# Statistics of the last layer norm: four row tiles from VectorE to two accumulating ScalarE passes each

## The chip, the cores and the metric

The kernel runs on one core of one Trainium2 chip. Its time is the device time of one execution in microseconds (us), and the median of the runs is compared. The core has five engines with a queue of instructions each: TensorE (PE in the profile; PEld is its weight load), VectorE (DVE), ScalarE (ACT), GpSimd (POOL) and SyncE (SP), which here only issues DMA transfers. An engine works through its own queue in order and waits for the others by semaphores.

## What is computed

The kernel is one layer of a hybrid decoder trunk on a sequence of 1024 positions with 1024 channels, in float32. Two token mixers and an output projection come first; they are not touched. The change concerns the end:

```python
def layer_norm(x, g, b):
    mu = jnp.mean(x, axis=-1, keepdims=True)
    var = jnp.mean(jnp.square(x - mu), axis=-1, keepdims=True)
    return (x - mu) * lax.rsqrt(var + LN_EPS) * g + b

def conv_ffn(h, w_up, dw_w, dw_b, w_down):
    u = causal_dwconv(h @ w_up, dw_w, dw_b)
    gate, val = jnp.split(u, 2, axis=-1)
    return (jax.nn.silu(gate) * val) @ w_down      # inner width 2816

h = layer_norm(DN_ALPHA * h + mix, ln1_g, ln1_b)
ffn = conv_ffn(h, w_up, dw_w, dw_b, w_down)
h = layer_norm(DN_ALPHA * h + ffn, ln2_g, ln2_b)   # the last norm, the kernel's output
```

## The kernel before, in words

A matrix product in float32 precision is done as three products of rounded operands: high part by high part (line 190), high by low (191) and low by high (192). So each weight tile is first cast by ScalarE into its high part (L1251 in the last stage), and then VectorE subtracts the high part from the original for the low part (L1252). The matmuls of lines 191 and 192 wait for that subtraction.

The last stage is `down()`, the product with `w_down`. It is done by Strassen's scheme in its seven-product form: the table `products` lists seven block products p = 0 to 6, each over NK = 11 steps k. A product adds up in four of the eight PSUM banks, X (`acc` in the profile) or Y (`sm`), one bank for each of four row blocks t of 128 positions; a step is 4 x 3 = 12 matmuls of 128x512. The function `load(p, k)` brings the operands of a step: the activations from scratch by SyncE (L1212), the weight block by SyncE (L1215), and, where a product needs a sum of two blocks, a second operand by GpSimd's queue (L1219) and an addition on VectorE (L1184). Then come the cast and the subtraction. The raw tiles, called `dr_1`, `dr_2` and so on, rotate through five buffers; the split tiles, called `w_dn<p>_<k>`, through six.

When a product is complete, a function of the table adds its banks to the residual rows. The rows lie in eight tiles of 128x1024: tiles 0 to 3 in `rows03`, tiles 4 to 7 in `rows47`; E is their first half of 512 columns, L their second. After product 1, `two(t)` completes half E of tiles 0 to 3 (L1272). After product 5, `four(t)` completes half L of the same tiles and ends them: `ln_out`. After product 6, `three(t)` completes half E of tiles 4 to 7 (L1269) and ends these. So tiles 0 to 3 are finished beside the matmuls of product 6, and tiles 4 to 7 as their banks come out at the end. In product 6 the last eight steps are done bank by bank, so that the four banks are complete one after another; the last four of its weight tiles (`last`) are loaded long ahead.

The last norm of a tile goes like this. When a half of the row is complete, `ln_part` takes its statistics (BN_STATS, L231, 128x512). `ln_stats` joins the two halves' statistics into mean and variance (BN_AGGR, L250), ScalarE takes the root of the variance plus eps (L251), and VectorE its reciprocal (L254). `ln_apply` goes over each half twice: minus mean, times gain (L258); times reciprocal root, plus bias (L261). A half of the result then leaves by SyncE (L1335).

The order of each engine's queue is not that of the code. The instructions are recorded by a layer that sorts them by priorities (`high_priority` raises those of the weight loads by 4000 and those of tile 7's norm by 200) and by its own estimate of when operands are ready; it also sets the waits. So an instruction that is taken out can move others.

Of the kernel before, what the change touches and what calls it, by code (L numbers as in the profile page):

```python
# [8 lines left out]
F32 = mybir.dt.float32  # L9
F32R = mybir.dt.float32r  # L10
AF = mybir.ActivationFunctionType
ALU = mybir.AluOpType
# [4 lines left out]
P = 128  # L17
D = 1024
T = 1024
HALF = 512  # L20
# [41 lines left out]
def kernel(  # L62
# [17 lines left out]
    V, A, G, TE, SY = nc.vector, nc.scalar, nc.gpsimd, nc.tensor, nc.sync  # L80

    def pool(name, bufs=1, **kw):
        return tc.tile_pool(name=name, bufs=bufs, reuse_waits="tile", **kw)
# [11 lines left out]
    def bank(which):  # L95
# [16 lines left out]
    eps = const.tile([P, 1], F32, name="eps")  # L112
# [3 lines left out]
        out=quads, in_=ident.rearrange("p (j h) -> p h j", j=4), axis=AX.X, op=ALU.add  # L116
# [113 lines left out]
    def ln_part(pl, t, st, q):  # L230
        return V.bn_stats(out=st[:, q, :], in_=t[:, q * 512 : (q + 1) * 512])  # L231

    def ln_stats(pl, tiles, name, sts=None, keep=None):

        n = len(tiles)
        if keep is None:
            mv = pl.tile([P, n, 2], F32, tag="ln_mv", bufs=2, name=f"mv_{name}")
            rs = pl.tile([P, n], F32, tag="ln_rs", bufs=2, name=f"rs_{name}")
        else:
            mv, rs = keep  # L240
        for i, t in enumerate(tiles):
            if sts:
                st = sts[i]
            else:
                st = pl.tile([P, 2, 6], F32, tag="ln_st", bufs=2, name=f"st_{name}{i}")
                for q in range(2):
                    part = ln_part(pl, t, st, q)
                    if keep is not None:
                        parts_of.append(part)
            V.bn_aggr(out=mv[:, i, :], in_=st)  # L250
        root = A.activation(out=rs, in_=mv[:, :, 1], func=AF.Sqrt, bias=eps)  # L251
        if keep is not None:
            in_order.append(root)
        V.reciprocal(out=rs, in_=rs)  # L254
        return mv, rs

    def ln_apply(t, mv, rs, i, g, b):
        one = V.scalar_tensor_tensor(  # L258
            out=t, in0=t, scalar=mv[:, i, 0:1], in1=g, op0=ALU.subtract, op1=ALU.mult
        )  # L260
        two = V.scalar_tensor_tensor(  # L261
            out=t, in0=t, scalar=rs[:, i : i + 1], in1=b, op0=ALU.mult, op1=ALU.add
        )
        return one, two
# [875 lines left out]
    def down(upp, dp):  # L1140
# [20 lines left out]
        ]  # L1161
        c4.append(upp.tile([P, HALF], F32, tag="s3", name="c4_last"))
        rs = [r[:, t * D : (t + 1) * D] for r in (rows03, rows47) for t in range(4)]
        sts = [dp.tile([P, 2, 6], F32, name=f"st_f{t}") for t in range(8)]
        g, b = (dp.tile([P, D], F32, name=n) for n in ("ln2_g", "ln2_b"))
        first_own = dp.tile([P, 2, D], F32R, tag="w", bufs=3, name="w_dn_own")

# [103 lines left out]
        def more(ps, r, cs, op):  # L1271
            V.tensor_tensor(out=r[:, cs], in0=r[:, cs], in1=ps, op=op)  # L1272
# [3 lines left out]

        def two(t):
            more(Y[t], rs[t], E, ALU.add)
            ln_part(dp, rs[t], sts[t], 0)

        def six(t):
            own(X[t], rs[t], L, ALU.subtract)
# [7 lines left out]

        def four(t):
            more(Y[t], rs[t], L, ALU.add)
            ln_part(dp, rs[t], sts[t], 1)
            ln_out(upp, t, rs[t], g, b, sts[t])

        def three(t):
            own(X[t], rs[4 + t], E, ALU.add)
            ln_part(dp, rs[4 + t], sts[4 + t], 0)
            ln_out(upp, 4 + t, rs[4 + t], g, b, sts[4 + t])

        products = (
            (X, True, one),
            (Y, True, two),
            (X, False, six),
            (Y, True, seven),
            (X, False, five),
            (Y, False, four),
            (X, False, three),
        )
# [15 lines left out]
                    block(banks[t], ws[k], t, first, k)  # L1325
                then(t)

    def ln_out(dp, t, r, g, b, st):

        with tc.high_priority(offset=200 if t == 7 else 0):  # L1330
            mv, rstd = ln_stats(dp, [r], f"f{t}", [st])
            halves = [slice(q * HALF, (q + 1) * HALF) for q in range(2)]
            for cs in halves:
                ln_apply(r[:, cs], mv, rstd, 0, g[:, cs], b[:, cs])
                SY.dma_start(out[t * P : (t + 1) * P, cs], r[:, cs])  # L1335

    warm(46)
# [3 lines left out]
    with pool("rows0") as pl:  # L1341
        rs = [pl.tile([P, D], F32, name=f"r0_{t}") for t in range(4)]
# [20 lines left out]
    upp = ctx.enter_context(pool("up"))  # L1363
# [4 lines left out]
    ffn_stack.close()  # L1368
    dp = ctx.enter_context(pool("down", side="right"))
    down(upp, dp)  # L1370


# [98 lines left out]
```

## Time and profile before

| what | value |
|---|---|
| median of 3 runs | 1940.59 us (1940.09 to 1940.99) |
| profiled execution, its own time | 1940.01 us |
| span of the profile, first to last instruction | 1937.9 us |
| granted TensorE clock, mean | 0.999 |
| DVE busy, 1779 to 1790 us | 10.24 of 11.00 us |
| ACT busy, 1897 to 1938 us | 6.51 of 41.00 us |
| BN_STATS of the last norm (L231) | 16, 682 ns each |
| BN_AGGR of the last norm (L250) | 8, 202 ns each |

Rows of the timeline give start and duration in us, the engine, the line, the operation, the output and inputs by the program's names without numbers, and the count that is merged into the row; in brackets stands how long the engine sat idle before it and who ended that. Neighbours on an engine overlap a little, so the step from start to start is shorter than a duration. A row of the waits gives the total, the count and the longest in us. A row of a group gives busy us in total, mean ns of one, then idle time before them.

### The profile page before, as it was taken

To read this page: it belongs to the slowest core of one execution; us is meant where nothing else is said; L and a number is where in the kernel's file an instruction comes from. 1 tells how busy PE (TensorE), PEld (TensorE's weight loads), DVE (VectorE), ACT (ScalarE), POOL (GpSimd) and SP (SyncE) were. 2 spreads that over 40 slices of the span, in tenths; PEclk is the share of its full clock that TensorE was granted. 3 is DMA by queue.
4 is the path that set the end of the run, shared out by engine and by line. 5 is a ranking of instruction groups with operands and counts; after the bars stand their busy time and mean duration, and the time that the engine had idled before them with its cause. 6 is when DMAs were issued, how large, how long until landed. Compare 5 with 4: busy or idle time off the path is not lost.

```text
span 1937.9 us, 25802 instructions
## 1 busy us (share of the span) xinstructions
PE 1921.9 (99%) x9424; PEld 1570.3 (81%) x9424; DVE 1607.4 (83%) x2242; ACT 1084.2 (56%) x1626; POOL 217.1 (11%) x256
## 2 busy tenths in 40 slices
PE   9999999999999999999999999999999999999998
PEld 8888877788888788888888888888888888888886
DVE  7599999999887639899999546587788888889778
ACT  6676767763353366776765435365555555543542
POOL 1001010112300001111112040001000000122010
PEclk9999999999999999999999999999999999999999
DMA  6655555547356665656544644566455555479673
GB/s 218 219 172 201 173 205 177 166 166 270 130 182 222 211 207 183 202 180 212 176 168 163 213 151 131 181 243 228 163 168 185 179 182 186 157 281 360 198 245 112
DMA packets 127216, 376.27 MB, mean 194 GB/s; under 512 B 15184, under 2 KB 15728, under 8 KB 127088
## 3 DMA queue, kind: packets, MB, share of 16 engines
q1 hardware_dynamic: 107424, 318.48, 48.7%
q0 software_dynamic: 13184, 44.59, 6.6%
q10 hardware_dynamic: 6480, 11.55, 1.6%
q8 instruction: 74, 1.21, 0.3%
q14 instruction: 54, 0.44, 0.1%
HBM read 290.00 MB, written 84.56 MB: 193 GB/s over the span
## 4 chain that ended last, share of the span: by engine, by line
PE 79%; DVE 16%; ACT 2%; issue 2%; DMA 1%; POOL 0%; DVEq 0%; ACTq 0%; POOLq 0%
PE acc L192 18%; PE acc L191 18%; PE acc L190 18%; PE sm L190 7%; PE sm L191 7%; PE sm L192 7%; DVE c L558 6%; DVE x L511 2%; DVE w_c L161 2%; PE sm L647 1%; DMA st_wo<-wo 1%; PE sm L655 1%; PE sm L650 1%; DVE m L642 1%; DVE x L665 1%
## 5 line engine op out<-in xcount | busy, mean ns | idle before, releaser
L192 PE MATMUL acc<-hT_h,w_c 128*128 128x512 f32 x1000 | 391.4, 392 | 0.5 <-DVE w_c L161 0.5
L190 PE MATMUL acc<-hT_h,w_c 128*128 128x512 f32 x1000 | 391.1, 391 | 0.2 <-ACT zs L575 0.2
L191 PE MATMUL acc<-hT_l,w_c 128*128 128x512 f32 x1000 | 391.1, 391 | 0.0
L558 DVE SCALAR_TENSOR_TENSOR c<-v,pc,c 128x512 f32<-128x512 f32 x480 | 373.0, 803 | 7.0 <-ACT c L547 4.5
L190 PEld LDWEIGHTS acc<-hT_h,w_c 128*128 128x128 f32 x1000 | 187.8, 188 | 41.3 <-issue 1.9
L192 PEld LDWEIGHTS acc<-hT_h,w_c 128*128 128x128 f32 x1000 | 187.8, 188 | 40.9 <-issue 1.5
L191 PEld LDWEIGHTS acc<-hT_l,w_c 128*128 128x128 f32 x1000 | 187.8, 188 | 39.4 <-issue 1.1
L156 ACT CAST w_c<-st_c 128x1024 fp32r<-128x1024 f32 x128 | 133.8, 1046 | 111.2 <-PE acc L192 83.8
L626 POOL TENSOR_TENSOR ce<-ce,xbc 128x1024 f32<-128x1024 f32 x28 | 78.5, 2805 | 690.3 <-ACT ce L625 690.3
L1251 ACT CAST w_dn<-dr 128x1024 fp32r<-128x1024 f32 (+1 forms) x72 | 67.3, 942 | 73.4 <-DVE dr L1184 36.4
L190 PE MATMUL sm<-h1s,w_s 128*128 128x512 f32 x264 | 102.8, 389 | 0.5 <-ACT fuv L1094 0.5
L191 PE MATMUL sm<-h1s,w_s 128*128 128x512 f32 x264 | 102.7, 389 | 0.0
L192 PE MATMUL sm<-h1s,w_s 128*128 128x512 f32 x264 | 102.2, 389 | 0.0
L615 ACT ACTIVATE m<-ab,acs 128x128 f32<-128x128 f32 x256 | 78.3, 389 | 41.2 <-PE sm L647 39.1
L161 DVE TENSOR_TENSOR w_c<-st_c,w_c 128x1024 fp32r<-128x1024 f32 x62 | 78.9, 1273 | 17.6 <-ACT w_c L156 17.4
L511 DVE SCALAR_TENSOR_TENSOR x<-u,pc,x 128x512 f32<-128x512 f32 x96 | 78.6, 832 | 5.7 <-ACT x L509 5.6
L1252 DVE TENSOR_TENSOR w_dn<-dr,w_dn 128x1024 fp32r<-128x1024 f32 (+1 forms) x72 | 77.8, 1086 | 2.8 <-ACT w_dn L1251 2.6
L192 PE MATMUL acc<-h1b_h,w_ue 128*128 128x512 f32 x176 | 68.9, 395 | 0.3 <-DVE w_ue L161 0.3
L190 PE MATMUL acc<-h1b_h,w_ue 128*128 128x512 f32 x176 | 68.7, 390 | 0.0
L191 PE MATMUL acc<-h1b_l,w_ue 128*128 128x512 f32 x176 | 68.5, 389 | 0.0
L190 PE MATMUL sm<-h1b_h,w_s 128*128 128x512 f32 x176 | 68.5, 389 | 0.0
L191 PE MATMUL sm<-h1b_l,w_s 128*128 128x512 f32 x176 | 68.5, 389 | 0.0
(360 smaller groups left out, 4541.9 us busy)
## 6 DMA issues: line engine op xcount, KB each, us to landing
st_c<-wcol SPq DMA_DIRECT2D x128, 512.0 KB, 4.5
low_scr<-w_c SPq DMA_DIRECT2D x64, 512.0 KB, 2.9
w_c<-low_scr SPq DMA_DIRECT2D x64, 512.0 KB, 4.2
ab<-acs_scr SPq DMA_DIRECT2D x32, 512.0 KB, 4.2
dr<-wdown SPq DMA_DIRECT2D x55, 256.0 KB, 4.8
st_wo<-wo SPq DMA_DIRECT2D x24, 512.0 KB, 4.2
st_ue<-wup SPq DMA_DIRECT2D x22, 512.0 KB, 3.7
first_scr<-first ACTq DMA_DIRECT2D x44, 256.0 KB, 3.0
```

The lines of the kernel that those rows point to most:

```text
L156: casts.append(A.copy(w[:, 0, :], st))
L161: sub.tensor_tensor(out=w[:, 1, :], in0=st, in1=w[:, 0, :].bitcast(F32), op=ALU.subtract)
L190: TE.matmul(ps, wa(0), xa(0), start=start, stop=False, skip_group_check=more)
L191: TE.matmul(ps, wa(0), xa(1), start=False, stop=False, skip_group_check=more)
L192: TE.matmul(ps, wa(1), xa(0), start=False, stop=stop, skip_group_check=more)
L511: V.scalar_tensor_tensor(out=o, in0=u[:, k : k + HALF], scalar=pc[:, wc + k : wc + k + 1], in1=o, op0=ALU.mult, op1=ALU.add,)
L558: V.scalar_tensor_tensor(out=accs[i], in0=v[:, k : k + HALF], scalar=pc[:, wc + k : wc + k + 1], in1=accs[i], op0=ALU.mult, op1=ALU.add,)
L615: A.activation(out=m[:, h, :], in_=ab[:, h, :], func=AF.Relu, scale=-1.0, bias=acs[:, c, 8 * g + h : 8 * g + h + 1],)
L626: G.tensor_tensor(out=ce, in0=ce, in1=CT[:, cs].unsqueeze(1).to_broadcast([P, 8, P]), op=ALU.mult)
L642: V.tensor_tensor(out=m, in0=m, in1=cbm.unsqueeze(1).to_broadcast([P, 8, P]), op=ALU.mult)
L1251: A.copy(w[:, 0, cs], src)
L1252: V.tensor_tensor(out=w[:, 1, cs], in0=src, in1=w[:, 0, cs].bitcast(F32), op=ALU.subtract)
```

## The change

Tiles 0 to 3 no longer get BN_STATS and BN_AGGR on VectorE. Instead `ln_out` has ScalarE go over the finished row of 1024 twice. The first pass writes the row times −1/1024 to a scratch tile and adds it up in its accumulator, which gives minus the mean (L1337 of the changed kernel). The second pass squares the row plus that number and adds up the squares (L1340). The root is taken of the sum times 1/1024 plus eps (L1341); the reciprocal stays on VectorE (L1342). The two passes of `ln_apply` are now written in `ln_out` (L1344 and L1347), with "plus minus the mean" in place of "minus the mean". Tiles 4 to 7 keep their statistics as they were.

```diff
         def two(t):
             more(Y[t], rs[t], E, ALU.add)
-            ln_part(dp, rs[t], sts[t], 0)
...
         def four(t):
             more(Y[t], rs[t], L, ALU.add)
-            ln_part(dp, rs[t], sts[t], 1)
-            ln_out(upp, t, rs[t], g, b, sts[t])
+            ln_out(upp, t, rs[t], g, b)
...
-    def ln_out(dp, t, r, g, b, st):
+    def ln_out(dp, t, r, g, b, st=None):
...
+            if st is not None:
+                mv, rstd = ln_stats(dp, [r], f"f{t}", [st])
+                mean, op, rstd = mv[:, 0, 0:1], ALU.subtract, rstd[:, 0:1]
+            else:
+                sums = dp.tile([P, 3], F32, tag="ln_sums", bufs=2, name=f"sums_f{t}")
+                mean, op, square, rstd = sums[:, 0:1], ALU.add, sums[:, 1:2], sums[:, 2:3]
+                out_of = dp.tile([P, T + 32], F32, tag="u", bufs=3, name=f"sq_f{t}")
+                A.activation(
+                    out=out_of[:, :D], in_=r, func=AF.Identity, scale=-1.0 / D, accum_out=mean
+                )
+                A.activation(out=out_of[:, :D], in_=r, func=AF.Square, bias=mean, accum_out=square)
+                A.activation(out=rstd, in_=square, func=AF.Sqrt, bias=eps, scale=1.0 / D)
+                V.reciprocal(out=rstd, in_=rstd)
             for cs in halves:
-                ln_apply(r[:, cs], mv, rstd, 0, g[:, cs], b[:, cs])
+                V.scalar_tensor_tensor(
+                    out=r[:, cs], in0=r[:, cs], scalar=mean, in1=g[:, cs], op0=op, op1=ALU.mult
+                )
+                V.scalar_tensor_tensor(
+                    out=r[:, cs], in0=r[:, cs], scalar=rstd, in1=b[:, cs], op0=ALU.mult, op1=ALU.add
+                )
                 SY.dma_start(out[t * P : (t + 1) * P, cs], r[:, cs])
```

Three places in the queues show what moves. The first is VectorE's queue where product 1 has ended and product 2 has begun. `sm458` and `sm459` are the last two banks of product 1, `st_f0` to `st_f3` the statistics of tiles 0 to 3, `dr_25` and `w_dn2_2` the raw and the split tile of step 2 of product 2, `dr_26` and `w_dn2_3` those of step 3. Before:

```order
L1272 TENSOR_TENSOR rows03_14246<-rows03_14246,sm458_14243 128x512
L1272 TENSOR_TENSOR rows03_14246<-rows03_14246,sm459_14244 128x512
L231 BN_STATS st_f0_14258<-rows03_14246 128x6
L1184 TENSOR_TENSOR dr_25_14785<-dr_25_14785,c3_14245 128x512
L231 BN_STATS st_f1_14259<-rows03_14246 128x6
L231 BN_STATS st_f2_14260<-rows03_14246 128x6
L231 BN_STATS st_f3_14261<-rows03_14246 128x6
L1184 TENSOR_TENSOR dr_26_14804<-dr_26_14804,c3_14245 128x512
L1252 TENSOR_TENSOR w_dn2_2_14789<-dr_25_14785,w_dn2_2_14789 128x1024
L1252 TENSOR_TENSOR w_dn2_3_14808<-dr_26_14804,w_dn2_3_14808 128x1024
```

The same place in the changed kernel:

```order
L1272 TENSOR_TENSOR rows03_14246<-rows03_14246,sm458_14243 128x512
L1272 TENSOR_TENSOR rows03_14246<-rows03_14246,sm459_14244 128x512
L1184 TENSOR_TENSOR dr_25_14777<-dr_25_14777,c3_14245 128x512
L1184 TENSOR_TENSOR dr_26_14796<-dr_26_14796,c3_14245 128x512
L1252 TENSOR_TENSOR w_dn2_2_14781<-dr_25_14777,w_dn2_2_14781 128x1024
L1252 TENSOR_TENSOR w_dn2_3_14800<-dr_26_14796,w_dn2_3_14800 128x1024
```

The four statistics are gone; the second addition still stands ahead of the first subtraction. The second place is ScalarE's queue at the last weight tiles of product 6, `w_dn6_5` and `w_dn6_6`, each cast in two halves from `c4` and `dr`. Before:

```order
L1251 CAST w_dn6_5_15810<-c4_5_14254 128x512
L1251 CAST w_dn6_5_15810<-dr_76_15808 128x512
L1251 CAST w_dn6_6_15817<-c4_6_14255 128x512
L1251 CAST w_dn6_6_15817<-dr_77_15815 128x512
L251 ACT_TABLE_LOAD
L251 ACTIVATE rs_f0_15688<-mv_f0_15687,eps_95 128x1
```

And in the changed kernel, where `sums_f0` and `sums_f1` hold the sums of tiles 0 and 1, and `sq_f0` and `sq_f1` are the scratch tiles:

```order
L1337 ACTIVATE sq_f0_15679,sums_f0_15678<-rows03_14246 128x1024
L1340 ACTIVATE sq_f0_15679,sums_f0_15678<-rows03_14246,sums_f0_15678 128x1024
L1251 CAST w_dn6_5_15802<-c4_5_14254 128x512
L1251 CAST w_dn6_5_15802<-dr_76_15800 128x512
L1337 ACTIVATE sq_f1_15692,sums_f1_15691<-rows03_14246 128x1024
L1341 ACT_TABLE_LOAD
L1341 ACTIVATE sums_f0_15678<-sums_f0_15678,eps_95 128x1
L1251 CAST w_dn6_6_15809<-c4_6_14255 128x512
L1251 CAST w_dn6_6_15809<-dr_77_15807 128x512
L1340 ACTIVATE sq_f1_15692,sums_f1_15691<-rows03_14246,sums_f1_15691 128x1024
```

Three passes and the table load now stand ahead of the casts of `w_dn6_6`. The third place is the end of VectorE's queue, with tile 6's norm (`f6`) and tile 7's (`f7`); `acc455` is the last bank to be completed. Before:

```order
L254 RECIPROCAL rs_f6_15923<-rs_f6_15923 128x1
L1269 SCALAR_TENSOR_TENSOR rows47_14248<-rows47_14248,acc455_14240 128x512
L261 SCALAR_TENSOR_TENSOR rows47_14248<-rows47_14248,rs_f6_15923,ln2_b_14267 128x512 x2
L231 BN_STATS st_f7_14265<-rows47_14248 128x6
L250 BN_AGGR mv_f7_15959<-st_f7_14265 128x2
```

And in the changed kernel:

```order
L254 RECIPROCAL rs_f6_15915<-rs_f6_15915 128x1
L1347 SCALAR_TENSOR_TENSOR rows47_14248<-rows47_14248,rs_f6_15915,ln2_b_14263 128x512 x2
L1269 SCALAR_TENSOR_TENSOR rows47_14248<-rows47_14248,acc455_14240 128x512
L231 BN_STATS st_f7_14261<-rows47_14248 128x6
L250 BN_AGGR mv_f7_15951<-st_f7_14261 128x2
```

Tile 6's last pair has changed places with tile 7's addition. Elsewhere VectorE's additions and subtractions of product 2 change places by a row or two. On TensorE, at steps 9 and 10 of product 2, six high-part products are put ahead of the low-part ones, and around the first use of `w_dn6_6` one matmul changes places. The queues of GpSimd and SyncE stay as they were.

More of the change, by code (lines that the diff above doesn't have):

```diff
@@ L1163, in down @@
         rs = [r[:, t * D : (t + 1) * D] for r in (rows03, rows47) for t in range(4)]
-        sts = [dp.tile([P, 2, 6], F32, name=f"st_f{t}") for t in range(8)]
+        sts = {t: dp.tile([P, 2, 6], F32, name=f"st_f{t}") for t in range(4, 8)}
         g, b = (dp.tile([P, D], F32, name=n) for n in ("ln2_g", "ln2_b"))
@@ L1326, in down @@
                 then(t)
-    def ln_out(dp, t, r, g, b, st):
+    def ln_out(dp, t, r, g, b, st=None):
+        halves = [slice(q * HALF, (q + 1) * HALF) for q in range(2)]
         with tc.high_priority(offset=200 if t == 7 else 0):
-            mv, rstd = ln_stats(dp, [r], f"f{t}", [st])
-            halves = [slice(q * HALF, (q + 1) * HALF) for q in range(2)]
-            for cs in halves:
-                ln_apply(r[:, cs], mv, rstd, 0, g[:, cs], b[:, cs])
+            if st is not None:
[11 more added lines that the diff above has]
+                V.reciprocal(out=rstd, in_=rstd)
+            for cs in halves:
+                V.scalar_tensor_tensor(
[4 more added lines that the diff above has]
+                )
                 SY.dma_start(out[t * P : (t + 1) * P, cs], r[:, cs])
```

## The prediction

> **What bounds the kernel now.** I read the page first, for the engine that is never idle.
>
> ```profile
> span 1937.9 us, 25802 instructions
> PE 1921.9 (99%) x9424; PEld 1570.3 (81%) x9424; DVE 1607.4 (83%) x2242; ACT 1084.2 (56%) x1626; POOL 217.1 (11%) x256
> ```
>
> TensorE is busy for 99% of the span. So work taken off VectorE, or put on ScalarE, is worth something only where TensorE waits for it, or behind TensorE's last matmul. Next I read the view of waits, for TensorE from 1000 us to the end, which covers the whole FFN.
>
> ```profile
> PE acc L190 <- ACT w_wo L156: 1.0, 1, 1.0
> PE acc L191 <- DVE w_dn L1252: 0.7, 1, 0.7
> PE sm L190 <- ACT fuv L1094: 0.5, 1, 0.5
> PE acc L192 <- DVE w_ue L161: 0.3, 1, 0.3
> ```
>
> Only the second wait is on a down-projection weight (`w_dn`), the stage that the change touches. The timeline of TensorE places it in product 2 (the products are counted from 0), step k = 2:
>
> ```profile
> 1781.01 1.07 PE L190 MATMUL acc<-w_dn 128*128 128x512 f32 x4
> ...
> 1783.73 1.07 PE L190 MATMUL acc<-w_dn 128*128 128x512 f32 x4
> 1785.51 0.50 PE L191 MATMUL acc<-w_dn 128*128 128x512 f32 x1 [0.71 <-DVE w_dn L1252]
> ...
> 1787.45 1.07 PE L190 MATMUL acc<-w_dn 128*128 128x512 f32 x4
> ```
>
> A step of twelve matmuls takes 1783.73 − 1781.01 = 2.72 us; this one takes 1787.45 − 1783.73 = 3.72. So the wait costs 1.00 us in all. The four high-part products go out at 0.227 us each, so the fifth matmul could have gone at 1784.64. The timeline of VectorE shows what kept its operand:
>
> ```profile
> 1779.46 1.28 DVE L1272 TENSOR_TENSOR rows<-rows,sm 128x512 f32<-128x512 f32 x2
> 1780.66 0.69 DVE L231 BATCH_NORM_STATS2 st_f<-rows 128x6 f32<-128x512 f32 x1
> 1781.27 0.67 DVE L1184 TENSOR_TENSOR dr<-dr,c 128x512 f32<-128x512 f32 x1
> 1781.86 1.87 DVE L231 BATCH_NORM_STATS2 st_f<-rows 128x6 f32<-128x512 f32 x3
> 1783.65 0.67 DVE L1184 TENSOR_TENSOR dr<-dr,c 128x512 f32<-128x512 f32 x1
> 1784.24 2.55 DVE L1252 TENSOR_TENSOR w_dn<-dr,w_dn 128x1024 fp32r<-128x1024 f32 x2
> ```
>
> Four of the statistics that the change removes stand right ahead of the late subtraction at 1784.24. The end of the program is bound differently: the last matmul, then a chain on VectorE.
>
> ```profile
> 1927.99 0.15 DVE L254 RECIPROCAL rs_f<-rs_f 128x1 f32<-128x1 f32 x1
> 1929.09 0.69 DVE L1269 SCALAR_TENSOR_TENSOR rows<-rows,acc 128x512 f32<-128x512 f32 x1 [0.94 <-PE acc L192]
> 1929.70 1.41 DVE L261 SCALAR_TENSOR_TENSOR rows<-rows,rs_f,ln_b 128x512 f32<-128x512 f32 x2
> 1931.02 0.69 DVE L231 BATCH_NORM_STATS2 st_f<-rows 128x6 f32<-128x512 f32 x1
> 1931.74 0.21 DVE L250 BATCH_NORM_AGGREGATE mv_f<-st_f 128x2 f32<-128x12 f32 x1
> ...
> 1931.99 1.41 DVE L258 SCALAR_TENSOR_TENSOR rows<-rows,mv_f,ln_g 128x512 f32<-128x512 f32 x2
> 1933.32 0.15 DVE L254 RECIPROCAL rs_f<-rs_f 128x1 f32<-128x1 f32 x1
> 1933.51 1.42 DVE L261 SCALAR_TENSOR_TENSOR rows<-rows,rs_f,ln_b 128x512 f32<-128x512 f32 x2
> ```
>
> VectorE idles 0.94 us until the last bank is ready at 1929.09, and then does tile 6's last pair (L261, 1.32 us from start to next start) ahead of tile 7's own statistics. That pair sits on the path that sets the end, though it was ready at 1928.2.
>
> **The change part by part.** *Eight statistics and four aggregations leave VectorE.* Four statistics were at product 2. Now the two additions (L1184) follow the L1272 pair directly, and the subtraction follows them. What is late next is the second addition's operand: its weight half was issued at 1770.30 and landed 12.6 us later.
>
> ```profile
> 1770.30 0.43 SPq L1215 DMA_DIRECT2D dr<-wdown  x1
> ```
> ```profile
> dr<-wdown SPq DMA_DIRECT2D x1, 256.0 KB, 12.6
> ```
>
> So that addition starts at about 1782.95, not at 1783.65. Everything behind it moves up by 0.70: the subtraction ends at 1784.76 and TensorE goes on at 1784.81, against the possible 1784.64. The wait shrinks by 0.70 us; it does not vanish. **Term one: −0.70**, between 0 (the landing is later) and −1.00 (the load comes 0.2 earlier). The other four statistics and the aggregations, at 1899 to 1910, lie beside matmuls and are worth nothing by themselves.
>
> *VectorE's order at the end.* In the new order tile 6's last pair stands ahead of tile 7's addition, so it can fill the 0.94 us of idle time. From L1269's start to the last row's end it was 1934.93 − 1929.09 = 5.84 us; without the pair it is 1931.02 − 1929.70 = 1.32 less, of which 0.11 comes back because the statistics now wait for the addition itself (0.72 from start to start, like 1931.02 to 1931.74, where 0.61 was the step). **Term two: −1.21**, if VectorE is not late at the last bank.
>
> *Eight accumulating passes come to ScalarE.* This decides whether VectorE is late. The rows for a pass of 128x1024:
>
> ```profile
> L622 ACT ACTIVATE m<-m 128x1024 f32<-128x1024 f32 x32 | 33.7, 1054 | 0.2
> ...
> L1105 ACT ACTIVATE fo<-fug,pc 128x1024 f32<-128x1024 f32 x22 | 25.4, 1154 | 3.3 <-DMA b_scr<-fo 2.7
> ...
> L251 ACT ACTIVATE rs_f<-mv_f,eps 128x1 f32<-128x1 f32 x8 | 2.3, 295 | 25.6 <-DVE mv_f L250 19.5 <-DVE rows L261 6.1
> ```
>
> The first pass has a constant scale (like L622, 1.05 us), the second a per-row bias (like L1105 with its per-row scale, 1.15). No row shows an accumulator's output. I bound it by nothing and by one more 128x1 instruction (L251, 0.29 us) a pass, and take the middle, 0.15.
>
> The passes of tile 0 begin when its row is summed. ScalarE's queue around them holds the last two weight tiles of product 6, each cast in two halves:
>
> ```profile
> 1899.17 0.62 ACT L1251 CAST w_dn<-c 128x512 fp32r<-128x512 f32 x1 [1.58 <-PE sm L192]
> ...
> 1901.89 0.62 ACT L1251 CAST w_dn<-c 128x512 fp32r<-128x512 f32 x1 [1.58 <-PE acc L192]
> 1902.42 0.61 ACT L1251 CAST w_dn<-dr 128x512 fp32r<-128x512 f32 x1
> 1903.05 1.28 ACT L251 ACT_TABLE_LOAD   x1
> 1904.35 0.57 ACT L251 ACTIVATE rs_f<-mv_f,eps 128x1 f32<-128x1 f32 x2
> ```
> ```profile
> 1897.13 0.69 DVE L1272 TENSOR_TENSOR rows<-rows,sm 128x512 f32<-128x512 f32 x1 [1.45 <-PE sm L192]
> ...
> 1901.93 0.68 DVE L1252 TENSOR_TENSOR w_dn<-c,w_dn 128x512 fp32r<-128x512 f32 x1
> 1902.52 0.69 DVE L1252 TENSOR_TENSOR w_dn<-dr,w_dn 128x512 fp32r<-128x512 f32 x1
> ```
>
> With a free accumulator: row at 1897.85; two passes to 1900.1; the casts of k = 5 to 1901.2; tile 1's first pass to 1902.3; table load 1.28 to 1903.6; square root to 1903.9; first half cast of k = 6 to 1904.5 (1902.5 before). Behind that wait VectorE: subtraction 0.6, tile 0's last pair 1.3, second subtraction 0.6, to 1907.0. TensorE wants that second half here:
>
> ```profile
> 1910.53 0.39 PE L192 MATMUL acc<-w_dn 128*128 128x512 f32 x1
> ```
>
> Three and a half us are left, so these delays cost TensorE nothing. After that VectorE is full: tiles 1 and 2 take 2.83 each (two pairs of 1.32 and a reciprocal's 0.19), so 1912.7; tile 3's first pair and reciprocal to 1914.2; tile 4's addition 0.6 and tile 3's last pair 1.3 to 1916.1; tiles 4, 5 and 6 at 0.72 + 0.25 + 1.33 + 0.15 for the statistics and the first pair, 0.6 for the addition and 1.3 for the last pair bring tile 6 to its end at 1928.7. That is 0.35 ahead of the last bank. Three passes stand ahead of the anchor at 1904.5, so an accumulator that costs r makes VectorE late by 3r − 0.35: none at r = 0, 0.5 at r = 0.29. **Term three: +0.25**, the middle. All of this chain starts from TensorE's own matmuls, so it moves with term one.
>
> The Trainium skill, "ScalarE: Activation LUTs", section "What ACT_TABLE_LOAD costs", puts a table switch at 1.28 us and a drain of 1.38 us behind it. In this trace the load begins at 1903.05 and the next instruction stands at 1904.35, so there is no room for the drain, and I count 1.28. By the page the anchor would be 1.38 us later and the sum −0.3.
>
> *TensorE's own order* moves at steps k = 9 and 10 of product 2: six high-part products go ahead. They need product 3's first weight tile, cast here, some 5 us ahead of k = 9 (1787.45 + 6 x 2.72 = 1803.8); I count nothing.
>
> ```profile
> 1797.33 1.56 ACT L1251 CAST w_dn<-dr 128x512 fp32r<-128x512 f32 x2
> ```
>
> **Sum:** −0.70 − 1.21 + 0.25 = −1.66 us. The profiled execution took 1940.01 us, 2.1 more than its span, so it would take 1938.35. The median of the runs is 1940.59, 0.58 above it: **1938.9**.
>
> **The rivals.** *The wait in product 2 stays.* If the load that landed at 1782.9 is later once VectorE runs ahead, TensorE waits for it instead of for the statistics. For it: twelve us of landing time mean a crowded queue. Against it: it is issued before anything changes. Then −1.21 + 0.25, so 1939.6; chance 0.15.
>
> *The table switch costs twice its load.* The one switch now has the last weight cast and tile 0's root queued behind it. If the stream stops for as long again as the row of the load shows (1.28 us), VectorE is 1.3 us later and most of term two is eaten: −1.66 + 1.28, so 1940.2. Against it: the row, where the next instruction follows at once. Chance 0.09. The drain on the Trainium skill's page above would act in this way.
>
> *The accumulating pass is much dearer, and ScalarE becomes the bound of the last norm* (slower). Eight passes go through it one after another. Free, they and what stands between them end at about 1911.7, and VectorE asks for tile 3's root at 1914.1; so it is late by 8r − 2.5, less the 0.35. From r = 0.6 a pass the two gains are gone. At twice the pass (r = 1.1, a second sweep) VectorE is 6 us late: −1.9 + 6 = +4.1, so 1944.7. Every row shows one sweep a pass, and nothing shows an accumulator. Chance 0.07.
>
> *More is won:* the load lands earlier and r is 0, so −2.2: 1938.4; chance 0.05, apart from the forecast's 0.64.
>
> **How the numbers follow.** About 0.2% (3.9 us) is what a measurement of this kernel can tell from no change, so 1936.7 to 1944.5 counts as the same. Only the dear pass reaches beyond it, and no sum here does on the other side; I keep 0.03 for faster by what I have not seen, 0.04 for slower, and 0.93 for within. The range goes from 1937.9 (all won, less the 0.5 between the lowest run and the median) to 1941.0 (the second rival with r at 0.29, and as much spread).
>
> **What would show it.** Right: TensorE's wait on L1252 near 1785 is about 0.1 us; tile 6's last pair ends near the last matmul, and tile 7's statistics directly follow its addition; the span ends 5.8 − 1.2 = 4.6 us of VectorE work after that addition; the accumulating passes take 1.05 to 1.45 us. Wrong: a wait of 0.7 that has only changed its releaser; VectorE idle at tile 3's root behind ScalarE; a new wait of TensorE on the last weight tile.

## The result, and the profile after

The changed kernel takes 1938.45 us (median of 22 runs, 1937.36 to 1940.36). The kernel before, run beside it, takes 1941.10 us (22 runs, 1938.31 to 1942.89). The ratio is 0.9987, with an interval of 0.9981 to 0.9993, so the change is worth −2.5 us, between −3.7 and −1.4. A second set of runs gave 0.9987 again (0.9979 to 0.9996). The profiled execution took 1939.41 us.

First the engines' busy time, from the page of the changed kernel:

```profile
PE 1922.7 (99%) x9424; PEld 1571.0 (81%) x9424; DVE 1601.1 (83%) x2230; ACT 1093.0 (56%) x1642; POOL 215.8 (11%) x256
```

VectorE has 12 instructions and 6.3 us less, ScalarE 8.8 us more. ScalarE has 16 more instructions, not 8: each pass brings a second one, which we shall meet below. Neither sum says anything of the time, for TensorE is at 99% as before. So to the waits of TensorE from 1000 us on, whose first row is:

```profile
PE acc L191 <- DVE w_dn L1252: 0.9, 1, 0.9
```

The wait that the first term of the sum was to remove is still there (0.7 before). The timelines of TensorE and VectorE at that place show who ends it now:

```profile
1784.46 1.07 PE L190 MATMUL acc<-w_dn 128*128 128x512 f32 x4
1786.44 0.50 PE L191 MATMUL acc<-w_dn 128*128 128x512 f32 x1 [0.91 <-DVE w_dn L1252]
...
1788.40 1.08 PE L190 MATMUL acc<-w_dn 128*128 128x512 f32 x4
```
```profile
1782.11 0.69 DVE L1184 TENSOR_TENSOR dr<-dr,c 128x512 f32<-128x512 f32 x1
1784.56 0.69 DVE L1184 TENSOR_TENSOR dr<-dr,c 128x512 f32<-128x512 f32 x1 [1.76 <-DMA dr<-wdown]
1785.17 2.55 DVE L1252 TENSOR_TENSOR w_dn<-dr,w_dn 128x1024 fp32r<-128x1024 f32 x2
```

The four statistics are gone, and in their place VectorE stands idle for 1.76 us. It waits at the second addition for its weight half, which was issued at 1771.74 and, by the view of DMA issues, took as long as before to land:

```profile
dr<-wdown SPq DMA_DIRECT2D x1, 256.0 KB, 12.8
```

1771.74 + 12.8 = 1784.54, and the addition starts at 1784.56. The step takes 1788.40 − 1784.46 = 3.94 us, 1.22 over the 2.72 of an unhindered one; in the profile before it was 1.00 over.

The end of VectorE's timeline answers to the second term:

```profile
1928.38 1.42 DVE L1347 SCALAR_TENSOR_TENSOR rows<-rows,rs_f,ln_b 128x512 f32<-128x512 f32 x2
1930.05 0.69 DVE L1269 SCALAR_TENSOR_TENSOR rows<-rows,acc 128x512 f32<-128x512 f32 x1 [0.26 <-PE acc L192]
1930.77 0.69 DVE L231 BATCH_NORM_STATS2 st_f<-rows 128x6 f32<-128x512 f32 x1
...
1933.27 1.42 DVE L1347 SCALAR_TENSOR_TENSOR rows<-rows,rs_f,ln_b 128x512 f32<-128x512 f32 x2
```

Tile 6's last pair lies ahead of tile 7's addition, VectorE is done with it 0.26 us before the last bank is ready, and from that addition to the end it is 1934.69 − 1930.05 = 4.64 us, against 5.84 before. And ScalarE, where the new work is:

```profile
1898.86 1.06 ACT L1337 ACTIVATE sq_f<-rows 128x1024 f32<-128x1024 f32 x1 [0.31 <-issue]
1899.83 0.18 ACT L1337 ACTIVATION_READ_ACCUMULATOR sq_f<-rows 128x1 f32 x1
1900.05 1.15 ACT L1340 ACTIVATE sq_f<-rows,sums_f 128x1024 f32<-128x1024 f32 x1
1901.10 0.19 ACT L1340 ACTIVATION_READ_ACCUMULATOR sq_f<-rows,sums_f 128x1 f32 x1
1901.19 0.60 ACT L1251 CAST w_dn<-c 128x512 fp32r<-128x512 f32 x1
...
1902.23 1.06 ACT L1337 ACTIVATE sq_f<-rows 128x1024 f32<-128x1024 f32 x1
1903.19 0.18 ACT L1337 ACTIVATION_READ_ACCUMULATOR sq_f<-rows 128x1 f32 x1
1903.39 1.28 ACT L1341 ACT_TABLE_LOAD   x1
1904.68 0.29 ACT L1341 ACTIVATE sums_f<-sums_f,eps 128x1 f32<-128x1 f32 x1
```

The passes take 1.06 and 1.15 us, as rows without an accumulator do in the kernel before (1.05 and 1.15). The accumulator is read by an instruction of its own, 0.18 us. The instruction behind the table load starts as the load ends.

### The profile page after: what moved, and what is told of

It reads as the page before. It is cut to its first block, busy times and chain, and to the rows that moved or that the text cites. A ratio compares the mean times of both kernels' runs of the same rounds, so it can differ in the third digit from the quotient of the medians.

```text
span 1937.7 us, 25808 instructions
## 1 busy us (share of the span) xinstructions
PE 1922.7 (99%) x9424; PEld 1571.0 (81%) x9424; DVE 1601.1 (83%) x2230; ACT 1093.0 (56%) x1642; POOL 215.8 (11%) x256
## 3 DMA queue, kind: packets, MB, share of 16 engines
q8 instruction: 74, 1.21, 0.3%
## 4 chain that ended last, share of the span: by engine, by line
PE 82%; DVE 11%; DMA 3%; ACT 2%; issue 2%; SPq 0%; DVEq 0%; POOL 0%; ACTq 0%; POOLq 0%
PE acc L192 19%; PE acc L191 19%; PE acc L190 19%; PE sm L190 6%; PE sm L192 6%; PE sm L191 6%; DVE c L558 4%; PE sm L647 1%; DVE x L511 1%; DMA dr<-wdown 1%; PE sm L655 1%; PE sm L650 1%; DVE w_dn L1252 1%; PE acc L492 1%; DVE c L1184 1%
```

## The experiments

All ratios are to the kernel before, run beside the experiment on the same chip, with 95% intervals. **Theory:** the gain is the tail alone, and needs both parts of the change there, ScalarE's statistics and the new order; in product 2 the late load is the bound, with or without the statistics. **Rivals:** the statistics at product 2 do cost time; or the order alone brings the gain.

**The order alone.** The kernel before, all statistics on VectorE, with the last pair of each of tiles 4 to 6 put ahead of the next tile's addition:

```diff
-            own(X[t], rs[4 + t], E, ALU.add)
+            i = own(X[t], rs[4 + t], E, ALU.add)
+            if t:
+                issue_after(i, pairs[-1])
...
-                ln_apply(r[:, cs], mv, rstd, 0, g[:, cs], b[:, cs])
+                pairs.append(ln_apply(r[:, cs], mv, rstd, 0, g[:, cs], b[:, cs])[1])
...
```

> The kernel before, with one thing changed: tiles 4 to 6's last pairs are kept ahead of the next tile's addition, as in the changed kernel; all statistics stay on VectorE. Theory (the end gains by the order of VectorE's queue): from the start of tile 7's addition to the end of its last row 4.63 us instead of 5.84, so 1.2 us less than before in the median, and nothing changed in product 2. Rival (the order is free only because ScalarE took the statistics): VectorE, with eight statistics more, comes to tile 7's addition 1 us or more behind the last bank, and the time is that of before within 0.3 us.

Measured: 1940.60 us, ratio 0.9997 (0.9989 to 1.0006). The end of its VectorE timeline:

```profile
1930.26 1.41 DVE L261 SCALAR_TENSOR_TENSOR rows<-rows,rs_f,ln_b 128x512 f32<-128x512 f32 x2
1931.59 0.68 DVE L1269 SCALAR_TENSOR_TENSOR rows<-rows,acc 128x512 f32<-128x512 f32 x1
...
1934.80 1.41 DVE L261 SCALAR_TENSOR_TENSOR rows<-rows,rs_f,ln_b 128x512 f32<-128x512 f32 x2
```

From addition to end it is 4.62 us, as in the changed kernel, yet nothing is gained. The addition carries no bracket: VectorE came to it straight from the pair. The last matmul started at 1930.09, and VectorE can take the bank some 0.42 later (in the kernel before it was waiting and went on at 1929.09, with that matmul at 1928.67), so VectorE is 1.08 us late, as the rival had it. The order is worth something only to a VectorE that has time left.

**The order undone.** The changed kernel with tile 6's pair behind tile 7's addition again:

```diff
-            own(X[t], rs[4 + t], E, ALU.add)
+            i = own(X[t], rs[4 + t], E, ALU.add)
+            if t == 3:
+                for pair in pairs[-2:]:
+                    issue_after(pair, i)
...
```

> The changed kernel, with one thing put back: tile 6's last pair stands behind tile 7's addition, as before. Theory (the end's gain is this order alone): 5.84 us from tile 7's addition to its last row's end, 1.2 us more than the changed kernel, 1939.7. Rival (the gain comes from product 2): the time stays at the changed kernel's 1938.5 within 0.3 us.

Measured: 1940.10 us, ratio 0.9993 (0.9984 to 1.0001), 1.65 above the changed kernel's median and 1.1 above it by the means of the runs. Its tail:

```profile
1929.54 0.69 DVE L1269 SCALAR_TENSOR_TENSOR rows<-rows,acc 128x512 f32<-128x512 f32 x1 [1.70 <-PE acc L192]
1930.15 1.41 DVE L1355 SCALAR_TENSOR_TENSOR rows<-rows,rs_f,ln_b 128x512 f32<-128x512 f32 x2
...
1933.96 1.41 DVE L1355 SCALAR_TENSOR_TENSOR rows<-rows,rs_f,ln_b 128x512 f32<-128x512 f32 x2
```

VectorE now has 1.70 us of idle time at the last bank and leaves the pair for later; 5.83 us follow. The lateness at the last bank counts as well, so the fair measure of the tail runs from the start of the last matmul, here of the kernel before and of the changed kernel, to VectorE's end:

```profile
1928.67 0.39 PE L192 MATMUL acc<-last 128*128 128x512 f32 x1
```
```profile
1929.62 0.39 PE L192 MATMUL acc<-last 128*128 128x512 f32 x1
```

It is 6.26 us before, 6.12 with the order alone (from 1930.09), 6.25 with the order undone (from 1929.12) and 5.07 in the changed kernel. So in the tail the two parts are worth 1.2 us together, and next to nothing alone.

**The statistics late.** The kernel before, with the four statistics of product 2 taken after product 5:

```diff
-            ln_part(dp, rs[t], sts[t], 0)
...
-            more(Y[t], rs[t], L, ALU.add)
+            i = more(Y[t], rs[t], L, ALU.add)
+            issue_after(ln_part(dp, rs[t], sts[t], 0), i)
```

> The kernel before, with one thing changed: the first halves' statistics of tiles 0 to 3 are taken after product 5, not after product 1; nothing goes to ScalarE, and tile 6's last pair stays behind tile 7's addition. Theory 1 (the four statistics make the subtraction late): TensorE's wait in step 2 of product 2 falls to 0.2 us or less and the median by 0.7. Theory 2 (the weight block of step 3 lands too late, and the statistics only filled that time): the wait stays at 0.6 to 1.0 us, put down to the same subtraction, with VectorE idle before the addition of step 3 until that load, and the median is that of before within 0.3 us.

Measured: 1941.25 us, ratio 1.0001 (0.9992 to 1.0010). Product 2 lost 1.60 us without the statistics (TensorE's listed wait is 1.3), with VectorE idle for 2.21 us ahead of the second addition, ended by the load. The statistics cost elsewhere: a new wait of TensorE of 1.3 us in product 5, near 1884, and a tail of 7.08 us, since VectorE was behind at the end. So a wait is there without the statistics, for the load; the time says little, having three things in it.

**The statistics back.** The changed kernel, with the four statistics of product 2 on VectorE again, their results unused:

```diff
+        unused = [dp.tile([P, 2, 6], F32, name=f"unused{t}") for t in range(4)]
...
             more(Y[t], rs[t], E, ALU.add)
+            ln_part(dp, rs[t], unused[t], 0)
```

> The changed kernel, with the four statistics after product 1 put back on VectorE; their results are not used. Theory 1 (they make the subtraction late): TensorE's wait in step 2 of product 2 is 0.7 us or more longer than in the changed kernel's usual execution, median 1939.2. Theory 2 (the load of step 3 is what is late): no difference beyond 0.3 us, 1938.5.

Measured: 1938.90 us, ratio 0.9992 (0.9983 to 1.0001): by the medians 0.45 above the changed kernel, not to be told from it, and between the two theories. VectorE at product 2:

```profile
1782.66 1.88 DVE L231 BATCH_NORM_STATS2 unused<-rows 128x6 f32<-128x512 f32 x3
1784.90 0.69 DVE L1185 TENSOR_TENSOR dr<-dr,c 128x512 f32<-128x512 f32 x1 [0.36 <-DMA dr<-wdown]
```

Even behind three statistics the addition waits 0.36 us for its load. TensorE's listed wait is 1.6 us, 0.7 more than in the changed kernel's first profile, which was the sign of theory 1; but the load took 13.8 us here, and ended it. In this execution the statistics fit into time that VectorE would have stood idle. We shall see that it was not so in others.

**The loads out of the way.** What makes the load so late? In the same 40 us GpSimd's queue brings the rows 4 to 7, the gain and the bias, six times 512 KB, needed only much later. Both kernels were given a gate, a one-column copy on VectorE that holds these loads until product 3 or 4. The edit in `down()`, the same for both:

```diff
+        def gate(t, w):
+            V.tensor_copy(out=t[:, :1], in_=w[:, 0, :1].bitcast(F32))
...
-                if p == 2 and k % 2 and k < 8:
-                    load_row(4 + k // 2)
+                if p == 3 and 1 <= k <= 4:
+                    gate(rs[3 + k], w)
+                    load_row(3 + k)
...
+                    gate(g, w)
+                    gate(b, w)
```

For the changed kernel:

> The changed kernel, with GpSimd's loads of residual rows 4 to 7 and of gain and bias (3 MB) held back: each first waits for a copy of one column on VectorE behind a weight tile of product 3 or 4. Theory 2 (these loads crowd the weight block of step 3 of product 2, which lands 12 us after its issue): the block lands in about 5 us, TensorE's wait there is gone, and 1.0 us is won on the changed kernel, 1937.5. Theory 1 (the statistics were the cause, and they are gone already): no wait is left to win, 1938.5 within 0.3 us.

For the kernel before:

> The kernel before, with the same loads held back; all statistics on VectorE. Theory 2 (crowded loads make TensorE wait in product 2): the wait is gone although the four statistics are still there, and about 1.0 us is won on the kernel before. Theory 1 (the statistics make it wait): TensorE still waits 0.5 us or more near the start of product 2, and less than 0.4 us is won.

Measured: the changed kernel with the gate 1938.29 us, ratio 0.9985 (0.9976 to 0.9994); the kernel before with the gate 1939.44 us, ratio 0.9990 (0.9981 to 0.9998). Of the DMA issues between 1760 and 1800 us, the weight blocks and the rows in the changed kernel, and then the weight blocks with the gate:

```profile
dr<-wdown SPq DMA_DIRECT2D x13, 256.0 KB, 5.6
rows<-h_scr POOLq DMA_DIRECT2D x4, 512.0 KB, 8.3
do<-wdown POOLq DMA_DIRECT2D x7, 256.0 KB, 10.3
```
```profile
dr<-wdown SPq DMA_DIRECT2D x12, 256.0 KB, 4.4
do<-wdown POOLq DMA_DIRECT2D x6, 256.0 KB, 4.8
```

And TensorE at product 2 with the gate:

```profile
1779.87 1.07 PE L190 MATMUL acc<-w_dn 128*128 128x512 f32 x4
1782.59 1.07 PE L190 MATMUL acc<-w_dn 128*128 128x512 f32 x4
1785.31 1.07 PE L190 MATMUL acc<-w_dn 128*128 128x512 f32 x4
```

Every step is 2.72 us; the wait is gone. It is gone in the gated kernel before as well, with all four statistics still in VectorE's queue. So the statistics are not its cause by themselves: with the load in time there is room for them. What they cost when the load is late, the gate does not show. The two gated kernels differ by the tail (4.63 and 5.83 us) and by 1.15 us in the median. The gated changed kernel is the fastest of all by its profile (1936.47), but by its median only 0.4 below the changed kernel run beside it (1938.70), where 1.0 was expected; these runs cannot tell it from either. The gated kernel before is 1.95 below the kernel before run beside it (1941.39), also more than the expected 1.0.

**The addition out of the way.** The changed kernel, with the late addition of step 3 put behind the subtraction of step 2, and no load touched:

```diff
-                    add(w_st, w_st, c3[k])
+                    i = add(w_st, w_st, c3[k])
+                    if k == 3:
+                        issue_after(i, subs[-1])
...
```

> The changed kernel, in which the addition of step 3 of product 2 stands behind the subtraction of step 2 in VectorE's queue, instead of ahead of it. No load is touched. Theory (the wait in product 2 is TensorE waiting for a subtraction whose own operands are there, but which stands behind an addition whose load lands late): the wait of 0.9 us in step 2 is gone or at most 0.2, the addition of step 3 still waits for its load and ends in time for step 3, and the time is about 0.9 us below the changed kernel's (1937.5 by its median of 1938.45). Rival (product 2 needs the late load itself): the wait only moves to step 3, by as much or more, and the time is the changed kernel's, 1938.5. Both: from the last addition to the end 4.6 us.

Measured: 1937.79 us, ratio 0.9986 (0.9977 to 0.9994), beside the changed kernel's 0.9987. The view of waits has no wait on `w_dn` any more, but the steps 2, 3 and 4 take 3.21, 3.08 and 3.07 us: 1.20 over, as much as the changed kernel lost. VectorE's timeline shows why:

```profile
1782.80 0.69 DVE L1184 TENSOR_TENSOR dr<-dr,c 128x512 f32<-128x512 f32 x1
1784.74 1.23 DVE L1254 TENSOR_TENSOR w_dn<-dr,w_dn 128x1024 fp32r<-128x1024 f32 x1 [1.25 <-ACT w_dn L1253]
1785.88 0.68 DVE L1184 TENSOR_TENSOR dr<-dr,c 128x512 f32<-128x512 f32 x1
1787.81 1.23 DVE L1254 TENSOR_TENSOR w_dn<-dr,w_dn 128x1024 fp32r<-128x1024 f32 x1 [1.25 <-ACT w_dn L1253]
```

Addition, ScalarE's cast, subtraction, next addition: one behind the other they make 3.08 us a step (1782.80 to 1785.88), more than TensorE's 2.72. The time does not decide, for the median is nearer to the theory's 1937.5 and the ratio to the rival's. The steps do: as the rival had it, nothing is won in product 2, though its mechanism was not what happened. The loss did not move to one step but was spread over three, in waits too small for the list. A list of waits can get shorter with nothing gained; the starts of the steps tell.

**Both kernels again.** How far can one profile of each be trusted? The kernel before against itself, and a further profile of each kernel; the changed kernel a second time:

> The kernel before, unchanged, timed against itself. Theory (the two parts of the gain are the tail, 1.2 us, and scatter): ratio 1.000 within 0.0008; its profile shows the wait in product 2 between 0.7 and 1.6 us, like all runs with the statistics there so far, and 5.8 us from the last addition to the end. Rival (the first profile of before was a lucky one, and the statistics usually cost more): the wait in product 2 is 1.5 us or more, or a further wait of TensorE stands near 1884 us, in product 5.

> The kernel before once more, for a third profile: by the theory the wait in product 2 is between 0.7 and 1.6 us and nothing else is late until the last bank; by the rival it is 1.5 us or more, or a wait of over 0.5 us stands near 1884 us.

> The changed kernel once more, for a second execution to look at. Theory 1: the wait in step 2 of product 2 is under 0.3 us here, and the first execution's 0.9 was unusual. Theory 2: the wait is 0.6 to 1.0 us again, ended by the load. In both the end is 4.6 us from tile 7's addition to its last row's end.

> The changed kernel once more, for a third profile: the wait in product 2 is about 0.9 us, with VectorE waiting for the load ahead of the addition of step 3; 4.6 us from the last addition to the end; by the rival the wait is 0.5 us or less in some executions, which would make the first two unlucky ones.

Measured: the kernel before against itself 0.9998 (0.9989 to 1.0007); executions of 1941.54 (profiled), 1940.50 for before; 1938.35 (profiled) and 1937.73 for the changed kernel. In the second profile of before the place in product 2 looks like this on TensorE:

```profile
1781.80 1.07 PE L190 MATMUL acc<-w_dn 128*128 128x512 f32 x4
1784.75 1.19 PE L190 MATMUL acc<-w_dn 128*128 128x512 f32 x4
1787.05 0.50 PE L191 MATMUL acc<-w_dn 128*128 128x512 f32 x1 [1.11 <-DVE w_dn L1252]
...
1788.99 1.07 PE L190 MATMUL acc<-w_dn 128*128 128x512 f32 x4
```

The listed wait is 1.11 us, within the theory's bounds, but the two steps lost 0.23 + 1.52 = 1.75. The rival had half a point: the profile that the prediction was worked from was one with a small loss. VectorE in the same profile:

```profile
1783.39 1.88 DVE L231 BATCH_NORM_STATS2 st_f<-rows 128x6 f32<-128x512 f32 x3
1785.18 0.68 DVE L1184 TENSOR_TENSOR dr<-dr,c 128x512 f32<-128x512 f32 x1
```

The load of this addition landed at 1771.87 + 12.5 = 1784.37, so here the addition came 0.81 us after its load, straight behind the statistics. In the first and the third profile of before it came 0.75 and 0.23 after, with the order alone 0.25, with the statistics back at once. So, given when the load landed, the statistics held the addition up by 0 to 0.8 us. What product 2 lost in each profile, by the starts of its steps against 2.72 us each:

| profile | loss, us |
|---|---|
| before, three profiles | 1.00, 1.75, 1.68 |
| the order alone | 1.27 |
| the statistics back (unused) | 2.34 |
| changed, three profiles | 1.23, 1.20, 0.95 |
| the order undone | 1.53 |
| the statistics late | 1.60 |
| the addition out of the way | 1.20 |
| the passes twice (below) | 3.32 |
| gate, changed and before | 0, 0 |

With the statistics there the mean of the five is 1.61, without them that of the seven 1.58; but the 3.32 of one execution weighs on the second, and the medians are 1.68 and 1.23. The load of step 3 landed 4.6 to 7.7 us after the start of step 0 in these twelve. That scatter is larger than anything that the statistics could cost, so single profiles cannot settle their price.

**The passes twice.** The price of a dear pass, by doing each of the eight passes two times over:

```diff
-                A.activation(
+                for _ in range(2):
+                    A.activation(
...
-                A.activation(out=out_of[:, :D], in_=r, func=AF.Square, bias=mean, accum_out=square)
+                for _ in range(2):
+                    A.activation(
```

> The changed kernel with each of the eight accumulating passes done twice, the second over the first, so that the output is the same and ScalarE has 9.6 us more to do between 1899 and 1924 us. This prices the slower rival of the prediction, a pass that is dear. Theory (a pass costs 1.2 us, 0.18 of it for the accumulator, and the slack that hid it in the changed kernel is 1.3 us, from tile 3's root at 1913.8 to VectorE's reciprocal at 1915.1): the extra passes run that slack out and VectorE is late at every bank from tile 4's on; worked through both queues in the order that this kernel has, with the step from one start to the next of the changed kernel's profile, the last row ends about 4.7 us later: 1943.2. Rival (the prediction's formula for the dear pass, late by 8r - 2.85 in an unchanged order, with r = 1.38): 8.2 us later, 1946.6. Second rival (ScalarE has room for all of it, since it is busy for a small part of this stretch): at most 0.5 later, 1938.9.

Measured: 1941.10 us, ratio 1.0003 (0.9994 to 1.0012), so 2.65 us above the changed kernel; all three expectations missed. From the start of the last matmul (1930.66) to VectorE's end (1938.41) it is 7.75 us, against 5.07 in the changed kernel (1929.62 to 1934.69): 2.7 more, which is the measured difference. The kind of the loss was the theory's, for VectorE is late at the last bank by 1.5 us and the pair is behind the addition again; its size was not, and ScalarE's rows say why:

```profile
1903.17 1.06 ACT L1338 ACTIVATE sq_f<-rows 128x1024 f32<-128x1024 f32 x1
1904.13 0.18 ACT L1338 ACTIVATION_READ_ACCUMULATOR sq_f<-rows 128x1 f32 x1
1904.22 1.14 ACT L1342 ACTIVATE sq_f<-rows,sums_f 128x1024 f32<-128x1024 f32 x1
```

The first pass here steps on after 1904.22 − 1903.17 = 1.05 us, before the accumulator is read to the end. I take it that the next instruction is on another tile and does not need the sum; the rows do not name the tile. I had counted 1.19 for each. Likewise I had given VectorE the steps of dependent instructions (0.72, 0.25) where others now stand between them.

## Why the prediction was right and wrong

The time of 1938.45 us lies in the range and 0.45 from the forecast, and the forecast −1.66 us lies within the measured −3.7 to −1.4. The reasons held less well than the number. The 0.2% below which the prediction counted times as the same was too coarse for these runs, whose interval reaches 0.06% to either side.

**Term one (−0.70): the working failed, the size is open.** The step that failed is "So that addition starts at about 1782.95". It took the landing of the load from one profile, 4.6 us behind the start of step 0 of product 2 (1778.29). In the changed kernel it landed 5.5, 5.5 and 5.3 behind that start (1784.54, 1783.16 and 1782.91, against 1779.02, 1777.64 and 1777.62). So where the prediction left a loss of 0.30 us and a wait of 0.1, product 2 lost 1.23, 1.20 and 0.95, with waits of 0.91, 0.89 and 0.66: a wait that has changed its releaser, the prediction's own sign of being wrong. But the kernel before was off as well, and to the same side: its other two profiles lost 1.75 and 1.68, with the load 5.3 and 5.8 behind step 0 (1771.87 + 12.5 and 1771.12 + 12.8, against 1779.08 and 1778.12). The difference between three profiles of each is 0.35 us, less than they scatter. So it is neither shown that the term is −0.70 nor that it is nothing, and that the sum came out is partly luck. The gate shows that the wait needs a late load; it does not show that the statistics are free while the load is late.

**Term two held (−1.21; measured −1.20),** in each of the profiles: 5.84 in the three of before, 4.64 in the three of the changed kernel. Its condition, that VectorE is not late, was not a formality: with the same order and the statistics still on VectorE the tail gains 0.14 us and the time nothing that can be seen.

**Term three was mis-sized (+0.25; measured 0).** VectorE is 0.26 us early at the last bank; at r = 0 the prediction had 0.35 (the steps that it prints for tiles 4 to 6 add up to 12.45 us and so to 1928.55, not 1928.7, which would make it 0.54). Of the accumulator's 0.18 us, 0.14 comes on the path where the next instruction wants the sum (1898.86 to 1900.05 is 1.19 us); behind the second pass the cast starts after 1.14 us, as after any pass. Behind tile 1's first pass the table load starts after 1.16 us, at most 0.11 late. So the three passes ahead of the last cast cost 0.25 at most together, where the middle of the bounds gave 0.45. The 3.5 us of slack for the last weight tile stood: TensorE does not wait there.

**The table switch** costs its 1.28 us and no more: the load starts at 1903.39, the next instruction at 1904.68. So the second rival falls. The drain of 1.38 us that the Trainium skill, "ScalarE: Activation LUTs", section "What ACT_TABLE_LOAD costs", puts behind a load isn't in this trace either.

**The dear pass** (the slower rival) was far off: r is 0.14 at the most, and its break-even was 0.6. Its price was too high too: it gave +4.1 against the kernel before for a pass done twice, where the experiment is level with that kernel.

**The sum against the clock.** That the forecast is off by only 0.45 is luck in part: it was added to 1940.59, the median of three runs, and the 22 runs gave 1941.10, from where the same sum leads to 1939.4. The measured −2.5 us have three parts. The tail is −1.2 and shown.

The second part lies outside the span, which the prediction carried over as 2.1 us. The span is on record for nearly all runs: 2.0 to 2.15 us lie outside it in each of these runs of the kernel before, with the order alone and with the statistics late, but 1.65 to 1.8 in each run of the changed kernel and of its variants, except the gated one (1.8 to 2.0). So 0.36 us come from there. The gated kernel before has 1.7 as well, with all statistics on VectorE, so ScalarE's passes are not needed for it; what it is made of stays open, since no view reaches outside the span.

The rest is in the span ahead of the tail. From step 0 of product 2 to the last addition both kernels take 149.80 us plus the loss in product 2, in five of the six profiles to 0.01 (one of the changed kernel has 0.36 more), so behind product 2 nothing else differs. In the profiles the loss is 0.35 smaller and product 2 starts 0.4 earlier on average (1777.6 to 1779.0, against 1778.1 to 1779.1); both scatter by more. All runs together tell a little more: the mean span is 1938.9 in 96 runs of before and 1937.1 in 33 of the changed kernel. If the tail is 1.2 in all of them, 0.6 us are left, by my estimate with a standard error of 0.2. That fits term one better than the first rival, which leaves nothing here. The gate points the same way: it shortens the mean span of the kernel before by 1.6 us and that of the changed kernel by 0.8, and the gated spans differ by 1.2, the tail alone. But each of these gains is known to about half a microsecond only, so the removed statistics remain the likely source of this part, not the shown one.

## What to carry to other kernels

Before you take a stalled engine's neighbour in the queue for the cause, look for the operand that lands next, and in more than one profile: where a load lands just behind the work that you remove, most of the wait can stay under another name. Moving work off an engine pays at the end of the program by the idle time that it lets the engine fill, and only if the queue's order puts work there; here either half alone left the tail as it was. Check a wait that is gone against the starts of the steps, since a stall can be spread until no list shows it.

## What the runs showed of the hardware

An activation that adds up its output (`accum_out`) is two instructions: the pass, as long as without (1.06 and 1.15 us for 128x1024), and a read of the accumulator of 0.18 us. From start to start a pass takes 1.19 us where the next instruction needs the sum, and 1.05 in another place, where the next pass starts before the read has ended.

While six loads of 512 KB were under way from GpSimd's queue, the 256 KB block of step 3 on SyncE's queue took 12.3 to 14.3 us to land in twelve profiles, and 4.6 and 4.8 in the two with these loads held back. Blocks of 256 KB on GpSimd's own queue took 10.3 at the median in the changed kernel, and 4.8 with the gate.
